# Plain units of the two branch products put singly between the retention's work, and all merge gates kept in DRAM

## The chip, the core and the metric

The kernel runs on one core of one Trainium2 chip. Five engines work side by side, each in the order of its own instruction stream: TensorE (PE in the profile: matmuls into PSUM; PEld is its weight load), VectorE (DVE), ScalarE (ACT), GpSimd (POOL) and SyncE (SP, used for DMA issues only). DMAs are issued by SP, ACT and POOL and carried out by 16 DMA engines. The metric is the device time of one execution in microseconds, as the median of several.

## The reference

Two layers (`DEPTH = 2`) over one sequence of 512 frames of width 1024, all in float32. What matters here is the part of a layer with two branches and their merge:

```python
y_m = sigmoid(mo) * head_layernorm(mlstm(mq, mk, mv, mi, mf))         # branch A, 4 heads
rq4 = rope(rq); rk4 = rope(rk) * R_DK ** -0.5                          # branch B, 4 heads
hr  = retention_chunkwise(rq4, rk4, rv, log_gamma)
y_r = silu(rg) * head_layernorm(hr)
merged = sigmoid(gm) * (y_m @ w_bm) + sigmoid(gr) * (y_r @ w_br)
x = x + merged @ w_out
```

`mq` to `gr` are columns of one projection of the normalised input. A feed-forward block and an embedding block follow in each layer, and a last normalisation.

## The kernel before

All activations are kept transposed: 128 features by 512 frames to a tile, eight tiles to the model's width. Every float32 operand is split into a high and a low part (`fp32r`), and a product is three matmuls: high by high, high by low, low by high (`mm3`, L450). The weights pass once, in the order of `unit_list` (L152), and each step of the computation takes the next unit from it:

- A plain unit (`T8`, function `t8`, L455) makes one output tile from one block of 1024 x 128 weights: 8 x 3 matmuls of 512 columns into one PSUM bank.
- A `PAIR` unit (`run_pair`, L482) makes two output tiles by a scheme of seven products P1, P5, P6, P2, P3, P7, P4 over half-size blocks, each of 12 matmuls of 256 columns, in three PSUM banks a, b and c (P1, P6, P7 and P4 share bank a; P5 and P3 share c). ScalarE evicts P1, P5, P6 and P4 to the two scratch tiles `y`, VectorE adds P2, P3 and P7 to them (`pair_tiles`, L556). P4 is not run at once: it is put on the list `later`, and `flush` (L477) runs it after P5 of the next pair, in the middle of the next plain unit (`k == 3`), or at the first row of an attention. Only then is the pair's result consumed.
- A `WIDE` unit (`run_wide`, L519) makes the retention's values of two heads.

Preparation of the weights: SP loads raw blocks into four buffers (`fill_raws`, L370); ScalarE rounds a block to its high part and VectorE subtracts it for the low part (`split`, L286), two pieces ahead of their use (`ready`, L440; `LOOK = 2`). A plain unit has one such piece of 1024 columns, a pair has pieces A, C and B of 1024 and D of 512 and some sums on VectorE. GpSimd forms further sums of weights from DRAM to DRAM, one step at a time as `pace` (L341) allows, from a credit that each unit adds to (`tick`, L345).

Scratch: `tmp` (L283) gives out tiles of 128 x 512 from one group of `NTMP = 6` slots. The pairs' `y`, the rotary work's `u` and `w` (L1082), the scores' `p`, the gates and the buffers of DRAM transfers all come from it.

A planner orders each engine's instructions ahead of time: it takes them by their place in the program, lets an engine take a later one when an earlier one isn't ready by its own estimates, and gives evictions of pairs a higher rank (`ahead`, L552). On the chip each engine then runs that fixed order and waits by semaphores.

The order around the change, in each layer (L1279 to L1332): the values of heads 0 and 1 (`rv_vals(0)`); four plain units of `y_m @ w_bm`; queries and keys of head 0 (`r_qk(0)`, two pairs, each followed by the rotary work); gate pair 2, `bm` units 4 and 5, gate pair 3, `bm` units 6 and 7; scores of head 0; `r_qk(1)`; attention of head 0 (`r_attend`, L1100); the fetch of head 1's values from DRAM (`rv_fetch`, L1212, issued by GpSimd into the buffers that the attention has just read); the first gate pair of head 0; the scores of head 1; and so on. `rv_split` splits the fetched values. `r_out` (L1120) makes a head's gate pairs, transposes the attention's result back and multiplies. After the attention of head 2 and the fetch for head 3 comes `r_qk(3)`, then eight plain units of the first half of `y_r @ w_br` (`br0`), the scores of head 3, and `r_out(2)`.

A merge gate of tiles 0 to 3 is made early by plain units (`gm_tile`, L1141) and stored to DRAM (`gm_spill`); `bm_tile` (L1286) loads it into scratch, multiplies the product's tile by it and stores the result (`bm_spill`). The gates of tiles 4 to 7 come from gate pairs 2 and 3 (`gm_gates`, L1133) and stay in their scratch tiles until `bm_tile` multiplies them in place.

Of the kernel before, what the change touches and what calls it, by code (L numbers as in the profile page):

```python
# [151 lines left out]
def unit_list(i):  # L152

    u = [("IF",)]

    def t8(w, col, row=0):
        u.append(("T8", w, row, col))

    def v(col):
        for k in range(4):  # L160
            u.append(("V", k, col))

    def pair(g, p):
        u.append(("PAIR", (i, g), p))

    def mqk(h):
        for d in range(2):
            t8("w_in", CQ + h * 256 + d * P)
        for d in range(2):
            t8("w_in", CK + h * 256 + d * P)  # L170

    def mo(h):
        for d in range(2):
            t8("w_in", CO + h * 256 + d * P)

    def rqk(h):
        for a in range(2):
            pair(f"rqk{h // 2 * 2}", h % 2 * 2 + a)

    def rg(h):  # L180
        for a in range(2):
            pair(f"rg{h // 2 * 2}", h % 2 * 2 + a)

    def full(w, col=0, row=0, lo=0, hi=8):
        for c in range(lo, hi):
            t8(w, col + c * P, row)

    mqk(0)
    v(CV)
    full("w_in", CGM, 0, 0, 2)  # L190
    mqk(1)
    mo(0)
    full("w_in", CGM, 0, 2, 3)
    mqk(2)
    mo(1)
    v(CV + 512)
    mqk(3)
    mo(2)
    full("w_in", CGM, 0, 3, 4)
    mo(3)  # L200
    u.append(("WIDE", (i, "rv0"), 0))
    full("w_bm", 0, 0, 0, 4)
    rqk(0)
    for p in (2, 3):
        pair("gm", p - 2)
        full("w_bm", 0, 0, 2 * p, 2 * p + 2)
    rqk(1)
    rg(0)
    u.append(("WIDE", (i, "rv2"), 0))
    rqk(2)  # L210
    rg(1)
    rqk(3)
    full("w_br")
    rg(2)
    rg(3)
    for p in range(4):
        pair("gr", p)
        full("w_br", 0, 1024, 2 * p, 2 * p + 2)
    full("w_out")

    def pairs(seq):
        for kind, b, p in seq:
            if kind == "f":
                t8("w_ff1", b * 1024 + 256 * p)
                t8("w_ff1", b * 1024 + 256 * p + P)
            else:
                pair(f"ff{b}", p)

    pairs(ff_order()[0])
    u.append(("PE", 0))  # L230
    pairs(ff_order()[1])
    u.append(("PE", 1))
    full("w_pe_gate")
    return u


def build(ctx, tc, ins, out):
# [25 lines left out]

    xs_dram = tc.dram_tile([KT, P, T], F32, name="x_spill")
    br_dram = tc.dram_tile([L, KT, P, T], F32, name="br_spill")
    gm_dram = tc.dram_tile([L, 4, P, T], F32, name="gm_spill")
    bm_dram = tc.dram_tile([L, KT, P, T], F32, name="bm_spill")
    rv_dram = tc.dram_tile([L, 2, NT, P, T], F32, name="rv_spill")

# [13 lines left out]
    def tmp(name, dt=F32):  # L283
        return cur["tmp"].tile([P, T], dt, name=name, tag="t", bufs=cur["ntmp"])
# [654 lines left out]
    for i in range(L):  # L939
# [129 lines left out]
        def m_back(h, gs, num):  # L1069
            gate_out(f"l{i}m{h}o", gs, num, [bcol(i, "gmn", 2 * h + v) for v in range(2)], ym, 2 * h)  # L1070

        def r_qk(h):
            nm = f"l{i}r{h}"
            qk = qk_tiles(nm)

# [14 lines left out]

            for a, bn in ((0, "brq"), (1, "brk")):
                pair_tiles(f"{nm}{bn}", xs, rope(a, bn))
            return qk

        def r_scores(h, qk):
# [15 lines left out]
        def r_gates(h, w, gs):  # L1111

            def consume(g):
                for d in range(2):
                    ac.activation(g[d], g[d], AF.Silu, bias=bcol(i, "brg", 4 * h + 2 * w + d), scale=SIGN[d])
                    gs[2 * w + d] = g[d]

            pair_tiles(f"l{i}r{h}o{w}", xs, consume)
# [14 lines left out]
        def gm_gates(p):  # L1133
            def consume(g):
                for d in range(2):
                    ac.activation(g[d], g[d], AF.Sigmoid, bias=bcol(i, "bgm", 2 * p + d), scale=SIGN[d])
                    gm[2 * p + d] = g[d]

            pair_tiles(f"l{i}bgm{p}", xs, consume)

# [98 lines left out]
                conv_evac(o, *a)  # L1239
        vv = mv_vals(0, xa, n1.c)  # L1240
        gct, gem = gate_cols(i, grow_c, grow_m)
        gm = {}
        for c in range(2):
            gm_tile(c, xa, n1)
        pt = m_scores(0, qk)
# [38 lines left out]
            nc.scalar.dma_start(t, ins[n])  # L1284

        def bm_tile(c):  # L1286
            if c < 4:
                gm[c] = tmp(f"l{i}gml{c}")
                nc.scalar.dma_start(gm[c], gm_dram[i, c])
            o = t8(ym, f"l{i}bm{c}")  # L1290
            g = gm.pop(c)
            ve.tensor_tensor(g, o, g, OP.mult)
            nc.scalar.dma_start(bm_dram[i, c], g)

        for c in range(4):
            bm_tile(c)
        qk = r_qk(0)
        for p in (2, 3):
            gm_gates(p)
            bm_tile(2 * p)  # L1300
            bm_tile(2 * p + 1)
        pt = r_scores(0, qk)
        qk = r_qk(1)
        num = r_attend(0, pt, vv)
        vv = rv_fetch(1)
        gs = {}
        r_gates(0, 0, gs)
        pt = r_scores(1, qk)
        rv_split(vv)
        yr = acts(cur["br"], f"l{i}yr0")  # L1310
# [7 lines left out]
        r_out(1, num, yr, gs)  # L1318
        num = r_attend(2, pt, vv)
        vv = rv_fetch(3)  # L1320
        qk = r_qk(3)
        for c in range(KT):
            o = t8(yr, f"l{i}br0{c}")
            t = tmp(f"l{i}brs{c}")
            ac.activation(t[:, :T], o, AF.Copy)
            nc.scalar.dma_start(br_dram[i, c], t[:, :T])
        pt = r_scores(3, qk)
        rv_split(vv)
        yr = acts(cur["br"], f"l{i}yr1")
        r_out(2, num, yr)  # L1330
        num = r_attend(3, pt, vv)
        r_out(3, num, yr)  # L1332
        mh, ml = [], []
# [365 lines left out]
```

## Time and profile before

| what | before |
|---|---|
| median of 3 runs | 2337.66 us (2335.55 to 2340.91) |
| profiled execution | 2338.24 us, its span 2336.5 us |
| TensorE busy | 2317.7 us (99%), 13664 matmuls |
| VectorE busy | 1722.3 us (74%) |
| ScalarE busy | 1224.1 us (52%) |
| GpSimd busy | 401.4 us (17%) |
| granted TensorE clock | 0.998 |
| DMA | 394.95 MB, mean 169 GB/s |

The span runs from the first to the last instruction of the profiled execution; a few microseconds of the time lie around it. A busy share is an average over the whole span. Matmuls are pipelined and their ends are modelled, so that each is drawn longer than the distance to the next one's start. A row of the waits names the waiting engine, its tile and line, who released it, and then the sum, the count and the longest. A row of a timeline gives start, duration, engine, line, operation, output and inputs, and in brackets the idle time before it and who ended it. Tile names begin with the layer (`l0`, `l1`) and the head (`r1` is head 1 of the retention, `m3` head 3 of the other branch); `o0` and `o1` are a head's two gate pairs, `brq` and `brk` its query and key pairs, `s` its scores, `a` its attention, `ot` the transposes back.

### The profile page before, as it was taken

How to read it: one execution, taken by the hardware profiler on the slowest of the kernel's cores; microseconds unless marked ns; L12 is line 12 of the kernel's file. 1: busy time of each engine (PE TensorE's matmuls, PEld its weight loads, DVE VectorE, ACT ScalarE, POOL GpSimd, SP SyncE). 2: the span in 40 equal slices, each digit the busy share in tenths (PEclk: the TensorE clock that was granted, in tenths of full speed). 3: DMA queues.
4: the chain of work that ended last, by engine and by line, in shares of the span. 5: the costliest groups of instructions: out<-in, count | busy, mean ns of one | idle time of the engine just before them, and what ended most of it. 6: DMA issues, size and time to landing. Idle time of an engine off the chain costs nothing.

```text
span 2336.5 us, 35728 instructions
## 1 busy us (share of the span) xinstructions
PE 2317.7 (99%) x13664; PEld 2055.3 (88%) x13664; DVE 1722.3 (74%) x2658; ACT 1224.1 (52%) x1771; POOL 401.4 (17%) x618
## 2 busy tenths in 40 slices
PE   9999999999999999999999999999999999999998
PEld 8888898898998898899888888998989988998997
DVE  7878767896665577678778777778957656776785
ACT  6756544554554445445557564454636445445464
POOL 3122212112114212112422221000000020000012
PEclk9999999999999999999999999999999999999999
DMA  6665886668688777777766666434443442333431
GB/s 214 166 172 155 249 230 183 195 176 224 176 239 253 197 205 191 206 203 189 212 177 172 154 178 196 145 121 151 129 138 114 157 154 99 127 109 94 136 122 55
DMA packets 150540, 394.95 MB, mean 169 GB/s; under 512 B 19344, under 2 KB 22800, under 8 KB 150368
## 3 DMA queue, kind: packets, MB, share of 16 engines
q1 hardware_dynamic: 99808, 247.50, 32.6%
q0 software_dynamic: 35152, 117.73, 22.9%
q10 hardware_dynamic: 15408, 27.43, 3.5%
q8 instruction: 107, 1.75, 0.3%
q14 instruction: 65, 0.53, 0.1%
HBM read 373.71 MB, written 123.73 MB: 213 GB/s over the span
## 4 chain that ended last, share of the span: by engine, by line
PE 84%; issue 6%; DVE 5%; DMA 2%; ACT 2%; POOL 1%; SPq 0%; ACTq 0%; DVEq 0%; POOLq 0%
PE l1f L451 2%; PE l0f L451 2%; PE l0f L452 2%; PE l1f L452 2%; PE l1f L453 2%; PE l0f L453 2%; PE l1br L451 1%; PE l0br L451 1%; PE l0br L453 1%; PE l1br L452 1%; PE l0br L452 1%; PE l1br L453 1%; PE l0pg L451 1%; PE l0pg L453 1%; PE l1bm L451 1%
## 5 line engine op out<-in xcount | busy, mean ns | idle before, releaser
L287 ACT ACTIVATE wh<-wr 128x1024 fp32r<-128x1024 f32 (+1 forms) x223 | 231.2, 1044 | 286.4 <-issue 62.9
L288 DVE TENSOR_TENSOR wl<-wr,wh 128x1024 fp32r<-128x1024 f32 (+1 forms) x221 | 272.4, 1234 | 73.7 <-ACT wh L287 73.5
L287 ACT ACTIVATE wh_B<-wr 128x1024 fp32r<-128x1024 f32 x100 | 105.9, 1059 | 149.8 <-PE l1bm L452 13.1
L288 DVE TENSOR_TENSOR wl_B<-wr,wh_B 128x1024 fp32r<-128x1024 f32 x100 | 122.0, 1220 | 20.8 <-ACT wh_B L287 20.8
L287 ACT ACTIVATE wh_C<-wr 128x1024 fp32r<-128x1024 f32 x76 | 80.3, 1057 | 64.4 <-issue 9.6
L287 ACT ACTIVATE wh_D<-wr 128x512 fp32r<-128x512 f32 x76 | 48.0, 631 | 124.8 <-DVE wr L433 57.2
L288 DVE TENSOR_TENSOR wl_A<-wr,wh_A 128x1024 fp32r<-128x1024 f32 x76 | 92.8, 1221 | 20.2 <-ACT wh_A L287 20.2
L288 DVE TENSOR_TENSOR wl_C<-wr,wh_C 128x1024 fp32r<-128x1024 f32 x76 | 94.3, 1241 | 16.1 <-ACT wh_C L287 15.7
L287 ACT ACTIVATE wh_A<-wr 128x1024 fp32r<-128x1024 f32 x76 | 80.0, 1052 | 47.2 <-PE l0f L452 6.7
L451 PE MATMUL l1f<-l1n2h,wh 128*128 128x512 f32 x256 | 99.9, 390 | 0.0
L451 PE MATMUL l0f<-l0n2h,wh 128*128 128x512 f32 x256 | 99.8, 390 | 0.0
L453 PE MATMUL l0f<-l0n2h,wl 128*128 128x512 f32 x256 | 99.7, 389 | 0.0
L453 PE MATMUL l1f<-l1n2h,wl 128*128 128x512 f32 x256 | 99.7, 389 | 0.0
L452 PE MATMUL l0f<-l0n2l,wh 128*128 128x512 f32 x256 | 99.6, 389 | 0.0
L452 PE MATMUL l1f<-l1n2l,wh 128*128 128x512 f32 x256 | 99.6, 389 | 0.0
L288 DVE TENSOR_TENSOR wl_D<-wr,wh_D 128x512 fp32r<-128x512 f32 x76 | 52.5, 690 | 36.9 <-ACT wh_D L287 35.8
L662 POOL TENSOR_TENSOR l1n3sum<-l1n3sum,l1n3sq 128x512 f32<-128x512 f32 x6 | 9.2, 1539 | 330.8 <-ACT l1n3sum L654 309.8
L430 DVE TENSOR_TENSOR wr<-wr,wr 128x512 f32<-128x512 f32 x76 | 52.2, 687 | 16.2 <-DMA wr<-wpairs 15.3
L453 PEld LDWEIGHTS l1f<-l1n2h,wl 128*128 128x128 f32 x256 | 48.0, 188 | 10.1
L453 PEld LDWEIGHTS l0f<-l0n2h,wl 128*128 128x128 f32 x256 | 48.0, 188 | 10.0
L452 PEld LDWEIGHTS l0f<-l0n2l,wh 128*128 128x128 f32 x256 | 48.1, 188 | 9.9
L452 PEld LDWEIGHTS l1f<-l1n2l,wh 128*128 128x128 f32 x256 | 48.1, 188 | 9.8
(5626 smaller groups left out, 8558.3 us busy)
## 6 DMA issues: line engine op xcount, KB each, us to landing
wr<-wstream SPq DMA_DIRECT2D x219, 512.0 KB, 4.5
wr<-wpairs SPq DMA_DIRECT2D x228, 256.0 KB, 3.0
wr<-wwide SPq DMA_DIRECT2D x24, 512.0 KB, 3.7
s0t<-wwide POOLq DMA_DIRECT2D x10, 512.0 KB, 5.6
s4t<-wwide POOLq DMA_DIRECT2D x10, 512.0 KB, 6.4
s12t<-wwide POOLq DMA_DIRECT2D x10, 512.0 KB, 5.4
s16t<-wwide POOLq DMA_DIRECT2D x10, 512.0 KB, 5.5
s1t<-wpairs POOLq DMA_DIRECT2D x16, 256.0 KB, 4.1
```

The lines of the kernel that those rows point to most:

```text
L287: a = ac.activation(hi_ap, src, AF.Copy)
L288: return a, ve.tensor_sub(lo_ap, src, hi_ap.bitcast(F32))
L430: ve.tensor_tensor(raws[n, "B"][:, Q:], kept.pop((n, "A"))[:, Q:], r[:, :Q], OP.add)
L451: te.matmul(o, sh, mh, start=first, stop=False)
L452: te.matmul(o, sh, ml, start=False, stop=False)
L453: cur["mm"] = te.matmul(o, sl, mh, start=False, stop=last)
L662: (add or gp).tensor_tensor(self.sum, self.sum, sq, OP.add)
```

## The change

The plain units of `y_m @ w_bm` and of the first half of `y_r @ w_br` are no longer run in blocks. The new order of a layer is: `bm` 0 and 1, `r_qk(0)`, gate pair 2, `bm` 2, gate pair 3, `bm` 3, scores 0, `bm` 4, first pair of `r_qk(1)`, `bm` 5, second pair, `bm` 6, attention 0 and fetch, first gate pair of head 0, `bm` 7, scores 1. Later: attention 2 and fetch, `br0` 0, first pair of `r_qk(3)`, `br0` 1 and 2, second pair, `br0` 3 and 4, scores 3, `br0` 5, `rv_split`, first gate pair of head 2, `br0` 6 and 7, `r_out(2)` with its other gate pair. `unit_list` gives the weights in the same order, and `r_qk` takes a function that it calls between its two pairs.

All eight merge gates now pass through DRAM: `gm_gates` stores its two tiles to `gm_spill`, which grows from 4 to 8 tiles per layer, and `bm_tile` loads every gate. Both DMAs are issued by ScalarE. The number of matmuls and of operations on VectorE and ScalarE is the same; each layer has four stores and four loads of 256 KB more.

```diff
@@ unit_list
-    full("w_bm", 0, 0, 0, 4)
+    def bm(c, n=1):
+        full("w_bm", 0, 0, c, c + n)
+
+    def br(c, n=1):
+        full("w_br", 0, 0, c, c + n)
+
+    bm(0, 2)
     rqk(0)
-    for p in (2, 3):
-        pair("gm", p - 2)
-        full("w_bm", 0, 0, 2 * p, 2 * p + 2)
-    rqk(1)
-    rg(0)
+    pair("gm", 0)
+    bm(2)
+    pair("gm", 1)
+    bm(3, 2)
+    pair("rqk0", 2)
+    bm(5)
+    pair("rqk0", 3)
+    bm(6)
+    pair("rg0", 0)
+    bm(7)
+    pair("rg0", 1)
     u.append(("WIDE", (i, "rv2"), 0))
     rqk(2)
     rg(1)
-    rqk(3)
-    full("w_br")
-    rg(2)
+    br(0)
+    pair("rqk2", 2)
+    br(1, 2)
+    pair("rqk2", 3)
+    br(3, 3)
+    pair("rg2", 0)
+    br(6, 2)
+    pair("rg2", 1)
     rg(3)
@@ build
-    gm_dram = tc.dram_tile([L, 4, P, T], F32, name="gm_spill")
+    gm_dram = tc.dram_tile([L, KT, P, T], F32, name="gm_spill")
@@ r_qk
-        def r_qk(h):
+        def r_qk(h, mid=None):
...
             for a, bn in ((0, "brq"), (1, "brk")):
                 pair_tiles(f"{nm}{bn}", xs, rope(a, bn))
+                if mid and not a:
+                    mid()
@@ gm_gates
                     ac.activation(g[d], g[d], AF.Sigmoid, bias=bcol(i, "bgm", 2 * p + d), scale=SIGN[d])
-                    gm[2 * p + d] = g[d]
+                    nc.scalar.dma_start(gm_dram[i, 2 * p + d], g[d])
@@ the layer
         def bm_tile(c):
-            if c < 4:
-                gm[c] = tmp(f"l{i}gml{c}")
-                nc.scalar.dma_start(gm[c], gm_dram[i, c])
+            g = tmp(f"l{i}gml{c}")
+            nc.scalar.dma_start(g, gm_dram[i, c])
             o = t8(ym, f"l{i}bm{c}")
-            g = gm.pop(c)
             ve.tensor_tensor(g, o, g, OP.mult)
             nc.scalar.dma_start(bm_dram[i, c], g)
-        for c in range(4):
-            bm_tile(c)
+        bm_tile(0)
+        bm_tile(1)
         qk = r_qk(0)
-        for p in (2, 3):
-            gm_gates(p)
-            bm_tile(2 * p)
-            bm_tile(2 * p + 1)
+        gm_gates(2)
+        bm_tile(2)
+        gm_gates(3)
+        bm_tile(3)
         pt = r_scores(0, qk)
-        qk = r_qk(1)
+        bm_tile(4)
+        qk = r_qk(1, lambda: bm_tile(5))
+        bm_tile(6)
         num = r_attend(0, pt, vv)
         vv = rv_fetch(1)
         gs = {}
         r_gates(0, 0, gs)
+        bm_tile(7)
         pt = r_scores(1, qk)
...
-        qk = r_qk(3)
-        for c in range(KT):
-            o = t8(yr, f"l{i}br0{c}")
-            t = tmp(f"l{i}brs{c}")
-            ac.activation(t[:, :T], o, AF.Copy)
-            nc.scalar.dma_start(br_dram[i, c], t[:, :T])
+        def br_tiles(*cs):
+            for c in cs:
+                o = t8(yr0, f"l{i}br0{c}")
+                t = tmp(f"l{i}brs{c}")
+                ac.activation(t[:, :T], o, AF.Copy)
+                nc.scalar.dma_start(br_dram[i, c], t[:, :T])
+
+        yr0 = yr
+        br_tiles(0)
+        qk = r_qk(3, lambda: br_tiles(1, 2))
+        br_tiles(3, 4)
         pt = r_scores(3, qk)
+        br_tiles(5)
         rv_split(vv)
+        gs = {}
+        r_gates(2, 0, gs)
+        br_tiles(6, 7)
         yr = acts(cur["br"], f"l{i}yr1")
-        r_out(2, num, yr)
+        r_out(2, num, yr, gs)
```

More of the change, by code (lines that the diff above doesn't have):

```diff
@@ L1241, in build @@
         gct, gem = gate_cols(i, grow_c, grow_m)
-        gm = {}
         for c in range(2):
```

## The prediction

> **What bounds the kernel now.** I read the page first (busy time by engine, then the span in 40 slices), then TensorE's waits, then the two stretches that the change rewrites, then the waits one by one on the timelines of TensorE, ScalarE and VectorE.
>
> ```profile
> span 2336.5 us, 35728 instructions
> PE 2317.7 (99%) x13664; PEld 2055.3 (88%) x13664; DVE 1722.3 (74%) x2658; ACT 1224.1 (52%) x1771; POOL 401.4 (17%) x618
> PE   9999999999999999999999999999999999999998
> PEclk9999999999999999999999999999999999999999
> ```
>
> TensorE is busy in every slice at the full granted clock, and the change removes and adds no matmul: the floor stays. What can move is only TensorE's idle time, and the list of its waits is short:
>
> ```profile
> PE l0r0o0c L501 <- ACT l0r0o0y L571: 2.0, 1, 2.0
> PE l1r0o0c L501 <- ACT l1r0o0y L571: 1.7, 1, 1.7
> ...
> PE l0r2o1a L501 <- DVE l0r2o1y L579: 0.7, 1, 0.7
> ...
> PE l1r3brqa L501 <- ACT l1r3brqy L569: 0.6, 1, 0.6
> PE l0r3brqa L501 <- ACT l0r3brqy L569: 0.6, 1, 0.6
> ...
> PE l1r2o1a L501 <- DVE l1r2o1y L579: 0.3, 1, 0.3
> ...
> 285.30:654.20 368.90, 365.63 (x2417) 335.88 (x2416) 277.31 (x416) 186.49 (x288) 69.23 (x103) 1.00 0.72 198
> 1442.60:1811.40 368.80, 366.18 (x2420) 336.35 (x2420) 278.19 (x417) 186.84 (x289) 12.03 (x20) 1.00 0.42 133
> ```
>
> The last two rows are the changed stretches, from the first `bm` unit to the first `br1` unit of each layer: length, then busy TensorE, weight loads, VectorE, ScalarE, GpSimd, then clock and DMA share. Six waits lie in them, 2.0 + 1.7 + 0.7 + 0.6 + 0.6 + 0.3 = 5.9 us, and the two rows' own idle agrees (3.27 + 2.62 = 5.9). Idle understates a stall, since a matmul's modelled end lies behind the start of the next:
>
> ```profile
> 402.62 0.28 PE L501 MATMUL l0r0o0a<-l0xsh,wh_B 128*128 128x256 f32 x1
> 402.74 0.28 PE L502 MATMUL l0r0o0a<-l0xsl,wh_B 128*128 128x256 f32 x1
> ...
> 403.33 0.40 PE L452 MATMUL l0r1s<-l0r1ql,l0r1kh 128*128 128x512 f32 x1
> 403.56 0.39 PE L453 MATMUL l0r1s<-l0r1qh,l0r1kl 128*128 128x512 f32 x1
> 405.90 0.38 PE L501 MATMUL l0r0o0c<-l0xsh,wh_C 128*128 128x256 f32 x1 [1.95 <-ACT l0r0o0y L571]
> ```
>
> Two matmuls of 512 columns start 0.23 us apart although each is drawn 0.39 us long (256 columns: 0.12 and 0.28), so each wait costs 0.16 us more than it shows: 5.9 + 6 x 0.16 = 6.9 us (0.3%). That is the most that the change can gain.
>
> **What each wait is made of.** In the first pair after `attend(0)` TensorE waits for ScalarE to evict product P5, and ScalarE was busy waiting for the four value tiles fetched from DRAM:
>
> ```profile
> 402.91 1.30 ACT L287 ACTIVATE l0r1vh<-l0r1vl 128x512 fp32r<-128x512 f32 x2 [0.84 <-DMA l0r1vl<-rv_spill]
> 404.95 0.63 ACT L287 ACTIVATE l0r1vh<-l0r1vl 128x512 fp32r<-128x512 f32 x1 [0.74 <-DMA l0r1vl<-rv_spill]
> 405.49 0.36 ACT L571 ACTIVATE l0r0o0y<-l0r0o0c 128x256 f32<-128x256 f32 x1
> ...
> 403.14 1.19 DVE L288 TENSOR_TENSOR wl_B<-wr,wh_B 128x1024 fp32r<-128x1024 f32 x1
> ...
> 391.40:406.00 14.60, 12.65 (x76) 10.76 (x74) 13.60 (x25) 8.36 (x15) 5.14 (x9) 1.00 0.52 174
> ```
>
> The fourth row shows a second cause: the pair's weights B got their low half only at 403.14 + 1.19 = 404.33, because VectorE was busy 13.60 of 14.60 us with the rotary work of head 1. With B late, TensorE's order leaves P6 (two matmuls done, the third, which needs the low half, due at 402.86) and P2, does three of the next scores and then goes to P3, which needs the late eviction. In `rqk3` it is ScalarE again, behind a fetched tile:
>
> ```profile
> 527.35 0.63 ACT L287 ACTIVATE l0r3vh<-l0r3vl 128x512 fp32r<-128x512 f32 x1 [0.69 <-DMA l0r3vl<-rv_spill]
> ```
>
> **The change, part by part.** A plain unit is 24 matmuls of 512 columns, 24 x 0.227 = 5.45 us (0.23 above, 45.0 us for eight units and a product below) of TensorE, and leaves VectorE and ScalarE nearly free: over the block of eight `br0` units VectorE is busy 45%, over the pairs behind it 72%:
>
> ```profile
> 545.20:590.20 45.00, 45.00 (x206) 37.49 (x205) 20.41 (x25) 14.04 (x19) 10.50 (x16) 1.00 0.85 216
> 594.10:616.80 22.70, 21.97 (x186) 21.70 (x185) 16.40 (x26) 13.47 (x24) 3.91 (x6) 1.00 0.72 187
> ```
>
> (1) `br0` unit 0 now stands between `attend(2)` with its fetch and the first `rqk3` pair. The splits of the fetched tiles wait behind 5.45 us of matmuls that need no eviction; the late landing was worth 0.6 us. Both waits go: 2 x (0.6 + 0.16) = -1.5 us.
>
> (2) `br0` units 6 and 7 stand between the two gate pairs of head 2: 10.9 us in which VectorE catches up before the product that waited for its add. -(0.7 + 0.16) - (0.3 + 0.16) = -1.3 us. What is late next there is nothing that the rows show.
>
> (3) `bm` unit 6 stands ahead of `attend(0)`, so head 1's rotary work starts 5.45 us sooner against the attention and the B weights (late by 404.33 - 402.86 = 1.5 us) are ready. P6 and P2 then run whole, 24 matmuls of 0.12 us = 2.9 us from 402.62, and P3 is due at 405.5 instead of 403.8. The eviction still ends at 405.49 + 0.36 = 405.85: 0.4 us stay of 2.0 + 0.16. The fetch itself is not moved, so I do not take the whole: -(2.1 - 0.4) - (1.9 - 0.4) = -3.2 us. From both sides: 0 if ScalarE's order moves with it, -4.0 if the landing comes 0.4 us sooner.
>
> (4) Four more gates per layer are stored and fetched by way of ScalarE's queue, 16 transfers in all. Issue costs 0.33 us each, 16 x 0.33 = 5.3 us of an engine that is idle 48% of the time: nothing on the path. The fetch and the two stores hold scratch slots, of which there are six:
>
> ```profile
> L1289 ACTq DMA_DIRECT2D l0gml<-gm_spill x4: 326/330/396, 245.8 to 271.3; - x4
> DMA to landing us min/median/max: 2.6/5.6/8.9
> ...
> L1293 ACTq DMA_DIRECT2D bm_spill<-l1gml x4: 326/326/327, 1449.0 to 1465.3; - x4
> DMA to landing us min/median/max: 2.0/2.1/4.0
> ...
> L1326 ACTq DMA_DIRECT2D br_spill<-l0brs x8: 326/326/333, 553.8 to 591.8; - x8
> DMA to landing us min/median/max: 4.7/5.0/5.3
> ```
>
> Before, the loads of gates 0 to 3 were issued 14 us or more ahead of their use. Unit `bm` 2 now follows gate pair 2 as unit 4 did before, and there the key's rotary scratch is given back late:
>
> ```profile
> 335.68 0.40 PE L451 MATMUL l0bm<-l0ymh,wh 128*128 128x512 f32 x1
> ...
> 339.08 0.69 DVE L1086 TENSOR_TENSOR l0r0brku<-l0r0brku,l0r0brkw 128x512 f32<-128x512 f32 x1
> ...
> L1289 ACTq DMA_DIRECT2D l1gml<-gm_spill x4: 326/329/402, 1403.1 to 1428.7; - x4
> DMA to landing us min/median/max: 2.0/2.7/2.7
> ```
>
> All six slots are taken until 339.08 + 0.69 = 339.8, 4.1 us into the unit; only then can its gate be asked for. It lands 2.6 to 8.9 us later in layer 0, and 2.0 to 2.7 in layer 1 (the last row). The multiply waits on VectorE, the store behind it on ScalarE, and the next evictions queue behind both. The unit with the product inside it has 2.8 us left, and the next pair runs 2.8 us before P6 wants its bank again, less 1.1 for multiply and eviction: 4.5 us of slack. That is 0 to 4.4 us in layer 0, 1.1 by the median, and nothing in layer 1. VectorE has room there, so I take 0.5.
>
> The Trainium skill, page DMA: Bandwidth & Descriptors, section Anatomy of one DMA (SWDGE path), fits one transfer as about 2.0 us and the bytes at 436 GB/s, an estimated 2.6 us for 256 KB. It matches layer 1's rows and is below layer 0's; by it this term would be zero and the sum 0.5 us lower.
>
> (5) `bm` unit 5 inside `rqk1` has a price that the blocks did not have. The first pair's P4 is flushed in the middle of the unit, so the rotary scratch u, w, u, w is asked for before the second pair's y. Scratch is given out in program order:
>
> ```profile
> 663.88 0.69 DVE L1354 TENSOR_TENSOR l0bml<-l0bml,l0brl 128x512 f32<-128x512 f32 x1
> ...
> 669.63 0.38 ACT L571 ACTIVATE l0gr1y<-l0gr1c 128x256 f32<-128x256 f32 x1 [0.97 <-PE l0gr1c L503]
> 669.69 0.33 ACTq L1348 DMA_DIRECT2D l0brl<-br_spill  x1
> ...
> 320.56 0.37 ACT L581 ACTIVATE l0r0brqy<-l0r0brqa 128x256 f32<-128x256 f32 x1
> 326.62 0.74 DVE L1085 SCALAR_TENSOR_TENSOR l0r0brqw<-l0r0brqy,bc,l0cos 128x512 f32<-128x512 f32 x1
> ```
>
> The scratch of `brl` was last read at 664.57, yet the next load into scratch comes at 669.69, right behind the pair's second y, which precedes it in the program. The last two rows give the rotary work's own time: its last scratch, the second w, is taken 326.62 - 320.56 = 6.1 us after the eviction of P4. In `rqk1` the second pair's P1 must be evicted 4.9 us after it: half a unit, 2.7, and two products of 1.4, less 0.4 for the eviction and 0.2 for P4's own tail. It costs 6.1 - 4.9 = 1.2 us if VectorE is as full as there, nothing if the unit frees it, and I allow twice that, 2.5, where the unit's own store still holds a slot. I take 1.2 per layer, the case that the rows show: +2.4 us. `rqk3` has two units between its pairs, so there it costs nothing.
>
> Sum: -1.5 - 1.3 - 3.2 + 0.5 + 2.4 = -3.1 us. The profiled execution took 2338.24 us (span 2336.5 and 1.7 around it), 0.6 above the median of the runs, 2337.66. From the median: 2334.6 us. A measurement of this kernel tells about 0.2%, 4.7 us, from no change; the sum is inside that.
>
> **Rivals.** First, all six waits go and none comes: 2337.66 - 6.9 = 2330.8 us. For it: every wait stands where a plain unit is put, and VectorE and ScalarE have room. Against it: the fetch of `attend(0)` is not moved. It is faster once 4.7 of the 6.9 us are kept.
>
> Second, slower: the scratch slots. If a y must take the slot of a store that has not landed, each such place costs the landing less the 1.4 us of slack, 5.0 - 1.4 = 3.6 us by the stores of `br0` in layer 0. The places are three per layer: gates 6 and 7, the second pair of `rqk1`, the second pair of `rqk3`. Three in layer 0 are +10.8; with the -6.0 of (1) to (3) that is 2342.5, and with layer 1's three at 4.0 - 1.4 = 2.6 it is 2350. I put it at 2344. It decides from 10.7 us of new waits on. For it: six slots, and a stage that now keeps one of them for a gate all the time. Against: before, gates 4 to 7 sat in their slots for a whole pair and two units, which is longer.
>
> Third, the change moves the waits and not their sum: ScalarE's splits come ahead of evictions elsewhere, and the time is 2337.7. For it: the order within each engine is planned ahead, from transfer times that the real landings exceed (the 0.84 and 0.74 us above).
>
> **How the numbers follow.** The forecast of 2334.6 (its own range 2333.0 to 2337.0) has 0.36, the third rival 0.07; both are no change: 0.43. The first has 0.27, faster. The second has 0.30, slower, since its price has the widest bounds. The range reaches from the first rival, 2330.8, less 0.8 for the spread between runs, to 2344.5 and leaves out the second's upper part, under 0.2.
>
> **What would show it.** Right: TensorE's waits no longer list `r3brq` and `r2o1`, `r0o0c` stays under 0.6, and a wait at `r1brk`'s first eviction appears. (3) is wrong if `r0o0c` is still 2.0; (5) if `r1brk` shows no gap. The prediction fails if waits of ScalarE on `gm_spill`, `bm_spill` or `br_spill` end gaps of TensorE of several us.

## The result and the profile after

The changed kernel takes 2343.55 us in the median of 20 runs (2337.38 to 2347.3), the kernel before 2339.3 us beside it, also of 20: a ratio of 1.002, with an interval of 1.0013 to 1.0026. It is slower by 0.2%, 4.3 us by the medians, where 3.1 us less was forecast. The profiled execution took 2343.51 us, its span 2341.8: 5.3 us more than the span before. TensorE is as busy as it was; these are the page's first lines and TensorE's waits in the changed stretches:

```profile
span 2341.8 us, 35732 instructions
PE 2321.0 (99%) x13664; PEld 2056.8 (88%) x13664; DVE 1725.2 (74%) x2658; ACT 1225.4 (52%) x1771; POOL 402.2 (17%) x618
...
PE l0bgm3a L518 <- ACT l0bgm3y L586: 2.4, 1, 2.4
PE l0r0o0a L518 <- ACT l0r0o0y L586: 2.3, 1, 2.3
PE l1r3brqa L520 <- DVE wl_B L305: 1.3, 1, 1.3
PE l0r3brqa L520 <- DVE wl_B L305: 1.1, 1, 1.1
...
PE l0r1brkc L518 <- ACT l0r1brky L588: 0.5, 1, 0.5
PE l1r1brkc L518 <- ACT l1r1brky L588: 0.5, 1, 0.5
```

The six waits of before are gone in their old form; six others have come. With 0.16 us added to each, as in the prediction, layer 1 gains: 0.66 + 1.46 new against 1.86 + 0.76 + 0.46 old is -0.96 us. Layer 0 loses: 2.56 + 2.46 + 1.26 + 0.66 against 2.16 + 0.86 + 0.76 is +3.2, and each of its two long stalls has a second price. The next rows are the same view as the stretches of the prediction (length, busy time of TensorE, weight loads, VectorE, ScalarE, GpSimd, then granted clock, DMA share, GB/s), for two times two neighbouring pieces of 3.4 us:

```profile
333.66:337.07 3.41, 1.30 (x12) 1.09 (x10) 1.27 (x2) 0.17 (x1) 0.00 (x0) 1.00 1.00 371
337.08:340.48 3.40, 3.15 (x14) 3.15 (x15) 2.63 (x5) 2.23 (x5) 0.00 (x0) 0.50 0.61 234
...
401.93:405.34 3.41, 1.09 (x10) 0.89 (x9) 3.32 (x8) 2.18 (x5) 0.57 (x1) 1.00 0.82 218
405.35:408.75 3.40, 3.40 (x19) 3.40 (x18) 2.46 (x6) 2.40 (x5) 2.07 (x2) 0.50 0.76 271
```

Behind either stall the clock is granted at 0.50 for 3.4 us, so up to half of that, 1.7 us, is lost again: at most 3.2 + 2 x 1.7 = +6.6 in layer 0, and 5.6 with layer 1, against 5.3 by the spans. Before, no piece inside the kernel ran at half clock.

**The stall in gate pair 3 of layer 0.** VectorE and ScalarE, from their timelines:

```profile
335.80 0.69 DVE L1308 TENSOR_TENSOR l0gml<-l0bm,l0gml 128x512 f32<-128x512 f32 x1 [4.37 <-DMA l0gml<-gm_spill]
...
326.73 0.33 ACTq L1306 DMA_DIRECT2D l0gml<-gm_spill  x1
...
336.53 0.33 ACTq L1309 DMA_DIRECT2D bm_spill<-l0gml  x1
336.90 0.38 ACT L586 ACTIVATE l0bgm3y<-l0bgm3a 128x256 f32<-128x256 f32 x1 [3.92 <-DVE l0gml L1308]
...
DMA to landing us min/median/max: 2.6/2.8/9.0
```

Gate 2 is asked for at 326.73, when the slots come free, and lands 9.0 us later (the last row: issue to landing of those of the 16 gate loads whose landing the trace tells; this is the longest). VectorE waits 4.37 us for it, the store of the product behind it on ScalarE, and the pair's first eviction behind that store.

**The stall in the first gate pair of head 0, layer 0,** begins ten microseconds earlier, at another late transfer:

```profile
386.09 0.79 POOL L353 DMA_DIRECT2D s5t<-wpairs  x1 [5.67 <-PE l0r1brka L520]
...
386.34 0.33 SPq L404 DMA_DIRECT2D wr<-wpairs  x1
...
393.00 0.69 DVE L447 TENSOR_TENSOR wr<-wr,wr 128x512 f32<-128x512 f32 x1 [5.04 <-DMA wr<-wpairs]
393.62 0.74 DVE L1101 SCALAR_TENSOR_TENSOR l0r1brku<-l0r1brky,bc,l0cos 128x512 f32<-128x512 f32 x1
...
402.44 0.69 DVE L450 TENSOR_TENSOR wr<-wr 128x512 f32<-128x512 f32 x1
...
403.16 0.63 ACT L304 ACTIVATE wh_D<-wr 128x512 fp32r<-128x512 f32 x1 [2.77 <-DVE wr L450]
...
404.22 0.36 ACT L586 ACTIVATE l0r0o0y<-l0r0o0a 128x256 f32<-128x256 f32 x1
```

VectorE's order has the sum of a freshly loaded weight ahead of head 1's key rotation. The load was issued at 386.34, 0.25 us behind one of GpSimd's weight sums (the first row), and VectorE waits 5 us for it. All that is queued behind it moves: the rotation, then the sum for piece D at 402.44, ScalarE's rounding of D, and the eviction that TensorE waits for.

### The profile page after: what moved, and what is told of

Its sections match the earlier page's. It is cut to its first block, busy times and chain, and to the rows that moved or that the text cites. A ratio compares the mean times of both kernels' runs of the same rounds, so it can differ in the third digit from the quotient of the medians.

```text
span 2341.8 us, 35732 instructions
## 1 busy us (share of the span) xinstructions
PE 2321.0 (99%) x13664; PEld 2056.8 (88%) x13664; DVE 1725.2 (74%) x2658; ACT 1225.4 (52%) x1771; POOL 402.2 (17%) x618
## 4 chain that ended last, share of the span: by engine, by line
PE 87%; DVE 6%; issue 3%; DMA 2%; ACT 1%; POOL 0%; ACTq 0%; DVEq 0%; SPq 0%; POOLq 0%
PE l1f L468 2%; PE l0f L468 2%; PE l0f L469 2%; PE l1f L469 2%; PE l1f L470 2%; PE l0f L470 2%; PE l0br L468 1%; PE l0br L470 1%; PE l0br L469 1%; PE l1br L468 1%; PE l1br L470 1%; PE l1br L469 1%; PE l0pg L468 1%; PE l0pg L470 1%; PE l1wo L469 1%
## 5 line engine op out<-in xcount | busy, mean ns | idle before, releaser
L468 PEld LDWEIGHTS l0f<-l0n2h,wh 128*128 128x128 f32 x256 | 48.1, 188 | 9.8
```

The lines of the kernel that those rows point to most:

```text
L468: te.matmul(o, sh, mh, start=first, stop=False)
```

## The experiments

Each run was timed in five rounds (two_sums in one) against the kernel before on the same chip, most with 11 executions, gate_early with 5, dummy_after with 6 and two_sums with 7; "us" is the difference of the medians, in brackets the interval of the ratio. The table has TensorE's waits in us, layer 0 / layer 1, with "-" where none is listed, and the stretches of half clock inside the kernel. The columns are the pairs at which TensorE waits: `bgm3` is gate pair 3, `r1brk` head 1's key pair, `r0o0` the first gate pair of head 0, `r3brq` head 3's query pair, `r2o1` the second gate pair of head 2.

| run | us | bgm3 | r1brk | r0o0 | r3brq | r2o1 | half clock |
|---|---|---|---|---|---|---|---|
| before | 0 | - / - | - / - | 2.0 / 1.7 | 0.6 / 0.6 | 0.7 / 0.3 | 0 |
| changed | +4.3 [1.0013, 1.0026] | 2.4 / - | 0.5 / 0.5 | 2.3 / - | 1.1 / 1.3 | - / - | 2 |
| bm_only | +2.3 [0.9996, 1.0014] | 0.7 / - | 0.5 / 0.5 | 3.5 / - | 0.3 / - | 1.2 / 0.3 | 1 |
| br_only | +1.9 [1.0002, 1.002] | - / - | - / - | 2.1 / 2.7 | 1.1 / 1.3 | - / - | 1 |
| nosum_before | -3.9 [0.9975, 0.9992] | - / - | - / - | 1.8 / 1.4 | - / - | 0.3 / 0.4 | 0 |
| nosum_after | -4.1 [0.9975, 0.9992] | - / - | 0.5 / 0.5 | - / 0.2 | 0.8 / 1.1 | - / - | 0 |
| gate_early | +13.0 [1.0037, 1.0062] | 5.5 / 2.1 | 0.5 / 0.5 | 3.3 / - | 1.3 / 1.1 | 0.2 / - | 3 |
| br0_later | +4.6 [1.0009, 1.0027] | 0.5 / - | 0.6 / 0.5 | 2.3 / - | 0.2 / - | 1.9 / 0.3 | 1 |
| bm5_out | +1.5 [0.9994, 1.0013] | 2.3 / - | - / - | 1.4 / 1.4 | 1.1 / 1.0 | - / - | 1 |
| sums_paused | +5.4 [1.0014, 1.0031] | - / - | 4.2 / 0.5 | - / - | 1.2 / 1.2 | 0.3 / - | 2 |
| dummy_before | +4.5 [1.0007, 1.0025] | - / - | - / - | 1.5 / 2.0 | 0.5 / - | 0.9 / 0.3 | 1 |
| dummy_after | +10.6 [1.003, 1.006] | 2.3 / - | 0.7 / 1.6 | 3.1 / - | 1.5 / 1.0 | 0.3 / - | 3 |
| one_copy | +4.5 [1.001, 1.0027] | 2.3 / - | 1.0 / 0.5 | 0.7 / - | 1.1 / 1.3 | - / - | 1 |
| two_sums | +8.1 [1.0026, 1.0051] | 1.7 / 1.6 | 0.5 / 0.5 | 2.7 / - | 1.4 / 0.9 | - / - | 2 |
| mix | -1.6 [0.9983, 1.0] | - / - | - / - | 0.9 / 0.8 | 0.7 / - | 1.3 / 0.3 | 0 |
| mix_paused | -1.1 [0.9987, 1.0004] | - / - | - / - | 0.9 / 0.9 | - / - | 0.3 / 0.3 | 1 |
| mix_bm | -3.5 [0.9977, 0.9995] | - / - | - / - | 0.3 / 0.8 | 0.6 / 0.8 | 0.9 / 0.3 | 0 |
| mix_br | +3.3 [1.0005, 1.0023] | - / - | - / - | 1.6 / 2.2 | 0.7 / - | 1.8 / 0.4 | 1 |

The waits are those of one execution, and the landings differ from one to the next: layer 1's `r0o0` is 2.7 us in br_only and 1.7 before, although layer 1 has the same order up to there. The time is the safer column.

### The two halves

```diff
 # bm_only: the br0 units as before
+    rqk(3); full("w_br"); rg(2); rg(3)
-    br(0); pair("rqk2", 2); br(1, 2); pair("rqk2", 3); br(3, 3); pair("rg2", 0); br(6, 2); ...
 # br_only: the bm units as before, gates 4 to 7 kept in scratch
+    bm(0, 4); rqk(0)
+    for p in (2, 3):
+        pair("gm", p - 2); bm(2 * p, 2)
+    rqk(1); rg(0)
```

> The bm half alone: the order of the eight bm units and the gates by way of DRAM as in the changed kernel, the eight br0 units in one block behind rqk3 as before. Theory A (the loss is made by late DMA landings in layer 0, at gate 2 of the merge and at the weights ahead of r0o0, each stall with a few us of half clock behind it): the whole loss stays, +4 to +7 us against the kernel before, with TensorE's waits at l0bgm3 and l0r0o0a over 2 us each and a half clock behind them, none in layer 1. Rival B (the loss comes from br0 unit 0 ahead of rqk3 and the other places of br0): within 2 us of the kernel before. Under both, the waits at r3brq stay as they were before (0.6 us each, on ScalarE).

> The br0 half alone: the order of the eight br0 units and of head 2's gates as in the changed kernel, the bm units in blocks and gates 4 to 7 kept in scratch as before. Theory A: r3brq gets worse by 0.6 to 0.8 us per layer, r2o1 better by 0.9 and 0.5, so -0.5 to +0.8 us, no difference to be measured. Rival B: +4 to +6 us. The step of the prediction that put -1.5 us on r3brq would give -2.8 with r2o1.

Theory A is met in neither run: the bm half should have kept +4 us or more and the br half should have cost nothing to be measured. By the medians each costs about half of the loss, +2.3 and +1.9 us, but bm_only's interval holds no change, so rival B is not ruled out by its time. In the bm half it is layer 0's `r0o0`, 3.5 us with a half clock behind; `bgm3` waits 0.7 us here, since gate 2 landed sooner. In the br half `r3brq` is worse as expected and `r2o1` is gone; its one half clock stands behind layer 0's `r0o0`, a place that this run does not change and where the kernel before waits about as long without one, so part of its +1.9 us may be chance.

### Without the weight sums

Of the two changed stretches, GpSimd's sums of weights from DRAM to DRAM run in that of layer 0 (GpSimd is busy 69 us of it and 12 of layer 1's, by the prediction's rows); in layer 1 they end ahead of it. In these two runs none is made, and another given block is loaded where a sum was.

```diff
-        return given[g, x] if x in GIVEN else sums[g, x]
+        return given[g, x] if x in GIVEN else given[g, "B12"]
...
-        dma = gp.dma_start(flat(block(g, x)[p:p + 1]), flat(block(g, MADE[x][a])[p:p + 1]), ...)
```

> The kernel before without the DRAM-to-DRAM weight sums on GpSimd's queue; another given block is loaded where a sum was, so the loads are the same and the output is not the reference's. This is the base for the next run. Both theories: -1 to -6 us against the kernel before (it is idle 18.8 us in all, and no matmul goes), with the r0o0c wait of layer 0 still there, since layer 1, which has few sums, has it as well (1.7 against 2.0 us).

> The changed kernel without the weight sums, in the same way (output not the reference's). Compare with the run without sums of the order before. Theory A: the waits of over 2 us at l0bgm3 and l0r0o0a are gone, no half clock in that stretch, layer 0 gains about what layer 1 gained (0.9 us), so -1 to -2 us against the order before. Rival C (the loss is the planned order on the engines and the scratch slots, whatever the DMA traffic): +4 to +6 us stay, and both waits stay over 2 us.

The loss is gone: 2334.86 us against 2335.13. So are both long stalls and the half clock, and layer 0 now looks as layer 1 does. The changed kernel's two stretches, and the same without sums:

```profile
285.00:660.00 375.00, 368.67 (x2410) 338.20 (x2410) 278.12 (x414) 186.94 (x288) 69.70 (x103) 0.99 0.72 202
1440.00:1815.00 375.00, 373.14 (x2442) 341.32 (x2441) 283.33 (x420) 190.09 (x291) 13.43 (x22) 1.00 0.43 141
```

```profile
285.00:660.00 375.00, 373.58 (x2455) 342.14 (x2454) 281.38 (x418) 191.11 (x294) 12.30 (x20) 1.00 0.45 142
1440.00:1815.00 375.00, 373.22 (x2454) 341.90 (x2453) 281.44 (x418) 191.03 (x293) 12.35 (x20) 1.00 0.44 142
```

That the loss needs the sums is shown. It is not a wait for a sum to be finished: the two late loads, of `gm_spill` and `wpairs`, carry none. Theory A's gain of 1 to 2 us is not shown: without late landings the change is worth 0.3 us, less than can be told. The waits moved and their sum stayed, which is the prediction's third rival.

### What makes gate 2 late, and whether asking earlier helps

```diff
 # gate_early
+        g2 = gate_load(2)
         gm_gates(2)
-        bm_tile(2)
+        bm_tile(2, g2)
```

> The changed kernel with the load of merge gate 2 issued ahead of gate pair 2 instead of behind it, one pair (about 8 us) earlier in the program. Theory A1 (the 2.5 us gap at l0bgm3 is the late landing of that gate): the gap there goes, with the half clock behind it, -2.5 to -4.0 us in layer 0 against the changed kernel, 2339.5 to 2341 us. Rival A2 (the gap is a scratch slot: the load holds one and the pair's y must wait for it, wherever the load stands): a gap of over 1 us stays in gate pair 2 or 3, and the time is within 1.5 us of the changed kernel.

A1 falls, and A2 with it: it is far worse than either. The load now takes the slot that the key's rotation needs, and the rotation waits for the store of the gate:

```profile
335.73 0.75 DVE L1102 SCALAR_TENSOR_TENSOR l0r0brkw<-l0r0brky,bc,l0sin 128x512 f32<-128x512 f32 x1 [8.22 <-DMA gm_spill<-l0bgm2y]
```

The store was issued at 326.89 and lands at the same time as the load did in the changed kernel, 335.7. In both orders one transfer must land within about a unit, the load or the store; with six slots the order chooses which. Layer 1 now stalls too (1.7 and 0.4 us), where no sums run: that is the price of the slots alone.

Can the sums step aside?

```diff
 # sums_paused
-        if at["step"] < len(steps) and at["credit"] >= 0:
+        if at["step"] < len(steps) and at["credit"] >= 0 and not cur.get("hold"):
...
+        cur["hold"] = i == 0
         gm_gates(2); bm_tile(2); gm_gates(3)
+        cur["hold"] = False
         bm_tile(3); ...; qk = r_qk(1, lambda: bm_tile(5))
+        cur["hold"] = i == 0
         bm_tile(6); ...; r_gates(0, 0, gs)
+        cur["hold"] = False
```

> The changed kernel, all sums made, but in layer 0 none is started from gate pair 2 to gate pair 3 and from the middle of rqk1 to the first gate pair of head 0; the credit that is saved up starts them behind. The theory as it stands after the earlier runs (a transfer of 256 KB that is due within one unit lands 5 to 9 us late while sums run, whether it is the gate's load, its store or a weight): both stalls of over 2 us (l0bgm3a, l0r0o0a) and their half clocks go, -5 to -8 us against the changed kernel, 2335.5 to 2338.5. Rival (a total of traffic in the layer is what counts, the pauses move the late landings to other places): within 2 us of the changed kernel.

Both stalls go, as the theory says, and the time stays, as the rival says. The sums that were saved up come between the pauses, and the same chain forms there, one pair earlier:

```profile
374.41 0.69 DVE L447 TENSOR_TENSOR wr<-wr,wr 128x512 f32<-128x512 f32 x1 [6.26 <-DMA wr<-wpairs]
...
377.72 0.63 ACT L304 ACTIVATE l0r1qh<-l0r1brqu 128x512 fp32r<-128x512 f32 x1 [4.00 <-DVE l0r1brqu L1103]
378.26 0.36 ACT L586 ACTIVATE l0r1brky<-l0r1brka 128x256 f32<-128x256 f32 x1
```

The opposite test puts the traffic into layer 1:

```diff
 # dummy_before, dummy_after: in layer 1, at the pace of the sums
+        dma = gp.dma_start(flat(spare[k // 2 % 8]), flat(given[g, "B12"][k % 2:k % 2 + 1]), **kw)  # 256 KB, every other one accumulating
 # one_copy: two plain copies of 512 KB at gate pair 2 of layer 1
+        cur["copies"] = [(0, wide, "B12", 0)] + [None] * 6 + [(1, wide, "B12", 1)] if i else []
 # two_sums: the same with accumulations into them, the last at the end of gate pair 2
+        cur["copies"] = [(1, wide, "B12", 1), (0, wide, "B22", 0, add)] + [None] * 5 + [(1, wide, "B22", 1, add)] if i else []
```

> The same 88 copies in layer 1 of the kernel before. Theory A: the old order has its loads and stores far enough ahead, so layer 1 becomes what layer 0 is there: +0 to +1.5 us (l1r0o0c, r3brq and r2o1 up by 0.1 to 0.4 us each), and the gap between the two orders grows from 4.3 to 8 us or more. Rival: the copies cost both orders alike.

> The changed kernel with the traffic of layer 0 put into layer 1 too: 88 more DRAM-to-DRAM copies and accumulations of 256 KB on GpSimd's queue, at the pace of the sums, from the first bm unit to the last gates of head 3; nothing reads them. Theory A: layer 1 now shows layer 0's stalls (at l1bgm3a and l1r0o0a, over 2 us, some with a half clock): +4 to +9 us against the changed kernel, and +8 to +13 against the kernel before; the run with the same copies in the order before is the base. Rival (layer 0's losses come from something else of that layer): +0 to +2 us, layer 1's waits as they were.

> The changed kernel with just two more copies of 512 KB from DRAM to DRAM on GpSimd's queue, in layer 1, where layer 0 has two such sums: one at the start of gate pair 2 and one at its end, right ahead of the load of gate 2 for unit bm 2. The 88 copies of 256 KB spread over layer 1 left l1bgm3a without a wait. Theory W (a wide copy that starts just ahead of a load that is due within one unit is what makes the stall, not the amount of traffic in the layer): layer 1's gate 2 lands 5 us or later after its issue (2 to 4.4 us in the changed kernel) and l1bgm3a waits 1 us or more. Rival (it takes the whole traffic of layer 0, weights, sums and spills together): it lands under 4.5 us and l1bgm3a has no wait over 0.3 us. The time tells little: +0 to +4 us against the changed kernel.

> The changed kernel with two whole wide sums on GpSimd's queue in layer 1, at the places of layer 0's: two copies of 512 KB from DRAM to DRAM and, behind them, two accumulations of 512 KB into them, the last right ahead of the load of gate 2; nothing reads the result. The plain copy of the last run left that load on time. Theory W2 (an accumulation, which reads its target and writes it again, is what holds the transfers up): layer 1's gate 2 lands 5 us or later and l1bgm3a waits 1 us or more. Rival (it takes the rest of layer 0's traffic as well): under 4.5 us and no wait over 0.3 us.

The 88 transfers of 256 KB miss what theory A expected: they cost the order before 4.5 us, not 0 to 1.5, and the gap between the two orders is 6.1 us, not 8 (dummy_after's six executions spread over 12 us, so the two are not told apart). Layer 1's `bgm3` and `r0o0a` stay without a wait; only its `r1brk` goes from 0.5 to 1.6 us. The profiled execution, the slowest of the six, also has a wait of 3.7 us at `l1bgm` with a half clock. It lies at 1280 us, ahead of the first added transfer at 1458, so the traffic does not make it. In one_copy the plain copies leave gate 2 on time. In two_sums, with the accumulations, the stall comes to layer 1, here on ScalarE:

```profile
1489.06 0.33 ACTq L1315 DMA_DIRECT2D l1gml<-gm_spill  x1
...
1498.15 0.33 ACTq L1318 DMA_DIRECT2D bm_spill<-l1gml  x1
1498.53 0.38 ACT L595 ACTIVATE l1bgm3y<-l1bgm3a 128x256 f32<-128x256 f32 x1 [3.16 <-DVE l1gml L1317]
```

So two wide sums, the last accumulation issued at 1488.00, about a microsecond ahead of a transfer due within one unit, are enough, and the amount of traffic in a layer is not. This rests on one execution of each. A narrow accumulation ahead of that load was not tried; in dummy_after one is issued 0.4 us behind it, and the load is on time. That a narrow one can do it too is suggested by the late weight ahead of layer 0's `r0o0`: the sum issued 0.25 us before it is one of 256 KB, and its issue takes 0.79 us, like the accumulations of two_sums (0.84) and unlike plain copies (0.53). The multiply began 8.4 us after the load's issue; the profile puts its wait down to a product that it does not read, so that landing is inferred.

### Steps 1, 2 and 5

```diff
 # br0_later
-    br(0)
     pair("rqk2", 2)
-    br(1, 2)
+    br(0, 3)
 # bm5_out
-    bm(5)
     pair("rqk0", 3)
-    bm(6)
+    bm(5, 2)
```

> The changed kernel with br0 unit 0 put behind the first pair of rqk3 instead of ahead of it (pair, br0 0 to 2, pair). Theory S (the unit ahead of the pair keeps the weight buffers, so that the pair's B weights get their low half too late): the waits for wl_B at r3brq (1.1 and 1.3 us) go, and at most the 0.6 us on ScalarE of the kernel before comes back: -0.6 to -1.4 us per layer, -1.2 to -2.8 us against the changed kernel. Rival (VectorE has too much to do after attend(2), whatever stands ahead of the pair): the waits for wl_B stay within 0.3 us.

> The changed kernel with bm unit 5 behind the second pair of rqk1 instead of between its two pairs. Step 5 of the prediction (scratch in program order makes the second pair's y wait): the gaps of 0.68 us at r1brk go in both layers, -1.4 us. The second reading (the gap at l0r0o0a comes from a late weight load that VectorE's order waits for, and that is late by the traffic): that gap can go either way in layer 0, 1.5 to 4 us, since the loads are not moved; if two units ahead of attend(0) instead of one make it vanish, VectorE's backlog was the cause and not the load.

Theory S holds for the wait and not for the time. In the changed kernel the unit ahead of the pair keeps a weight buffer until its last matmul, so ScalarE rounds B only then, and by then VectorE's order has the head's scaling and two splits ahead of B's low part:

```profile
538.46 1.06 ACT L304 ACTIVATE wh_B<-wr 128x1024 fp32r<-128x1024 f32 x1 [0.25 <-PE l0br L469]
...
538.54 1.92 DVE L834 TENSOR_SCALAR l0r2num<-l0r2num,l0r2mv,l0r2hv 128x512 f32<-128x512 f32 x4 [0.94 <-POOL l0r2hv L1126]
540.37 1.28 DVE L305 TENSOR_TENSOR l0r3vl<-l0r3vl,l0r3vh 128x512 fp32r<-128x512 f32 x2
541.58 1.22 DVE L305 TENSOR_TENSOR wl_B<-wr,wh_B 128x1024 fp32r<-128x1024 f32 x1
```

With the unit behind the pair, both waits for `wl_B` are gone, but `r2o1`'s are back (1.9 and 0.3), with the units 6 and 7 still between the gate pairs. VectorE of layer 1, in br0_later and then in the changed kernel:

```profile
1773.68 0.69 DVE L446 TENSOR_TENSOR wr<-wr,wr 128x512 f32<-128x512 f32 x1 [0.62 <-DMA wr<-wpairs]
1774.29 0.42 DVE L593 TENSOR_TENSOR l1r2o1y<-l1r2o1c,l1r2o1y 128x256 f32<-128x256 f32 x1
1774.62 1.22 DVE L304 TENSOR_TENSOR wl_C<-wr,wh_C 128x1024 fp32r<-128x1024 f32 x1
1775.75 0.42 DVE L595 TENSOR_TENSOR l1r2o1y<-l1r2o1a,l1r2o1y 128x256 f32<-128x256 f32 x1
```

```profile
1773.96 1.23 DVE L305 TENSOR_TENSOR wl_C<-wr,wh_C 128x1024 fp32r<-128x1024 f32 x1 [0.38 <-ACT wh_C L304]
1775.10 0.42 DVE L594 TENSOR_TENSOR l1r2o1y<-l1r2o1c,l1r2o1y 128x256 f32<-128x256 f32 x1
1775.43 0.68 DVE L447 TENSOR_TENSOR wr<-wr,wr 128x512 f32<-128x512 f32 x1
1776.03 0.42 DVE L596 TENSOR_TENSOR l1r2o1y<-l1r2o1a,l1r2o1y 128x256 f32<-128x256 f32 x1
```

In the first the sum of a weight, whose load has just not landed, stands ahead of both adds; in the second it stands between them, where it no longer waits. In layer 0 the same instruction waits 2.21 us in br0_later. So the wait goes with the place of that sum in VectorE's order.

Unit 5 behind the second pair takes `r1brk`'s gap away in both layers, as step 5 has it. The gap is not a wait for scratch, though. ScalarE in the changed kernel:

```profile
379.29 0.63 ACT L304 ACTIVATE l0r1qh<-l0r1brqu 128x512 fp32r<-128x512 f32 x1 [1.03 <-DVE l0r1brqu L1103]
...
379.83 0.36 ACT L588 ACTIVATE l0r1brky<-l0r1brkc 128x256 f32<-128x256 f32 x1
```

The second pair's P1 is evicted at 377.88, right behind its last matmul. What TensorE waits for is P5's eviction, which stands in ScalarE's order behind the rounding of head 1's query; ScalarE waits 1.03 us for VectorE's rotation there. Layer 1 shows the same. With unit 5 behind the pair, layer 0's `r0o0` shrinks to 1.4 us and layer 1's comes back with 1.4, though another unit now stands ahead of the attention: there ScalarE waits 1.94 us for a fetched value tile, and the eviction is behind its rounding.

### A version that beats both

```diff
 # mix_bm: the kernel before, except
-    for p in (2, 3): pair("gm", p - 2); full("w_bm", 0, 0, 2 * p, 2 * p + 2)
-    rqk(1)
+    pair("gm", 0); bm(4, 2); pair("gm", 1); bm(6)
+    rqk(1)
+    bm(7)                   # its gate alone by way of DRAM
 # mix_br: the kernel before, except
+    pair("rqk2", 2); br(0, 3); pair("rqk2", 3); br(3, 3); pair("rg2", 0); br(6, 2); pair("rg2", 1)
 # mix: both; mix_paused: mix with pauses of the sums at attend(0) to r0o0 and at head 2's gates
```

> Made of the parts that looked right: the bm units in the blocks of before, except that unit 7 stands behind rqk1, ahead of attend(0), with its gate by way of DRAM (the other gates as before); the br0 units 0 to 2 between the pairs of rqk3, 6 and 7 between the gate pairs of head 2. Theory A: r2o1's waits go (-0.9 and -0.5), layer 1's r0o0c goes (-1.9), r3brq -0.3 to +0.3 each, r1brk has no gap, l0bgm3 has none; layer 0's r0o0 between -2.1 and +2 us by the landing of the weights. In sum -5.4 to -1.3 us against the kernel before, 2333.5 to 2337.6. Rival (whatever stands ahead of attend(0) costs layer 0 as much as it gains layer 1, with a half clock): 0 to +2 us.

> The mixed order with pauses of the sums in layer 0 ahead of and at attend(0) to the first gate pair of head 0, and at head 2's gate pairs. Theory: the waits at l0r0o0a (0.9) and l0r2o1a (1.3) shrink by half or more, -1 to -2 us against the mixed order, 2334.5 to 2336.5. Rival (the pauses only move late landings): within 0.7 us of the mixed order.

> The bm half of the mixed order alone: bm 7 ahead of attend(0) with its gate by way of DRAM, everything else as in the kernel before. If the mixed order's gain is from this half: -1 to -2.5 us against the kernel before (r0o0's stalls of 2.1 and 1.9 become about 1.0 each). If it is from the br0 half: within 0.7 us.

> The br0 half of the mixed order alone: units 0 to 2 between the pairs of rqk3, 3 and 4 ahead of the scores, 5 behind them, 6 and 7 between the gate pairs of head 2; bm as before. The third rival of the prediction (waits move and their sum stays): r3brq's 0.75 go, r2o1's 0.5 to 2 stay, within 1 us of the kernel before. By the prediction's steps 1 and 2 it would be -2.8 us.

The bm half of the mix is the gain: 2335.54 us against 2339.03, a ratio of 0.9986 with 0.9977 to 0.9995, more than the 1 to 2.5 us expected. Its waits:

```profile
PE l0r2o1a L509 <- DVE l0r2o1y L587: 0.9, 1, 0.9
PE l1r3brqa L509 <- ACT l1r3brqy L577: 0.8, 1, 0.8
...
PE l0r3brqa L509 <- ACT l0r3brqy L577: 0.6, 1, 0.6
PE l1r0o0a L509 <- DVE l1r0o0y L587: 0.4, 1, 0.4
...
PE l1r0o0a L509 <- ACT l1r0o0y L577: 0.4, 1, 0.4
PE l0r0o0a L509 <- ACT l0r0o0y L577: 0.3, 1, 0.3
...
PE l1r2o1a L509 <- DVE l1r2o1y L587: 0.3, 1, 0.3
```

One unit ahead of `attend(0)` takes `r0o0` from 2.0 and 1.7 to 0.3 and 0.8, and one gate through DRAM, stored two pairs ahead of its use, makes no new wait. The br0 units between pairs lose by themselves even with unit 0 put right, 3.3 us where the rival had less than 1 and steps 1 and 2 a gain of 2.8: layer 1's `r3brq` gains, and layer 0's `r2o1` goes to 1.8 us with a half clock behind it. The pauses are worth nothing that can be told (-1.1 against -1.6 us for the mix without them), though `r2o1` in layer 0 falls from 1.3 to 0.3 us; mix_paused's half clock stands behind a wait of 3.5 us at `l1bgm`, far from the pauses.

## Why the prediction was wrong, step by step

By the waits of the two profiled executions the steps come to +1.2 for (1), -1.3 for (2), +0.3 and -1.9 for (3) in layers 0 and 1, +2.6 for (4) and +1.3 for (5), in sum +2.2 us where -3.1 was forecast; up to 3.4 of half clock, which the prediction put at nothing, come on top. The steps that failed most are (1), (3) in layer 0, (4) and the clock; all but (1) go away without the sums.

(1) Wrong. It looked at ScalarE, which the unit does relieve, and not at the weight buffers that the unit itself holds: instead of -1.5 the waits went to `wl_B`, 1.1 and 1.3 us, about +1.2 in all.

(2) Right in size (-1.3; both waits left the list), by luck, since its reason is wrong. VectorE had room before as well; what stood ahead of the add was a weight sum waiting for its load. br0_later has the same two units there and the wait.

(3) Right in layer 1, where the whole 1.7 + 0.16 went (1.5 was forecast). In layer 0 the wait became another of the same size, from a weight that landed 5 us late. The prediction named late landings for the gates and put none on the weights.

(4) The place, the chain and the mechanism are as it said; the term of 0.5 us was mis-sized. The landing was 9.0 us, at the upper end that it had noted (8.9), and the stall 2.4 + 0.16. With up to 1.7 of half clock that makes 4.3 us, and that this meets its bound of 4.4 is luck: the bound has no half clock in it, and it took the load to be asked for 4.1 us into the unit, where it was asked for at 1.7 (326.73; the unit's first matmul is at 325.01). Taking the median landing of a layer was the error: what counts is the landing at that moment, and two_sums points to an accumulating sum just ahead. By the estimate of the Trainium skill (page DMA: Bandwidth & Descriptors, section Anatomy of one DMA (SWDGE path)), 2.6 us, the gate would have been on time; layer 1's loads are near that, this one is 3.5 times as long. That section is about transfers issued by GpSimd, and these are issued by ScalarE.

(5) Right in place, in both layers, and gone in bm5_out; 0.66 us per layer instead of 1.2. The cause was not the scratch: the second w was taken 3.0 us after the eviction of P4 (376.71 against 373.70), not 6.1, and P1's eviction came on time. It was the first pair's rotary work on VectorE, which ScalarE's order waits for ahead of P5's eviction. The rows that it read as scratch in program order, the load at 669.69, show a load that stands behind an eviction in ScalarE's order, which is enough to explain it.

The rivals: the third holds once the sums are left out (-0.3 us). The second is what the scratch slots do in gate_early; that its 2344 lies beside the 2343.55 measured is luck, for none of the changed kernel's six waits is for the slot of a store. None counted the half clock, since before none of the stalls had one.

What stays open: why an accumulating sum holds a transfer up where a plain copy does not, and whether a narrow one is enough; why the added traffic costs the order before 4.5 us although its listed waits hardly grow; and the 0.1% that the br0 half costs, of which the waits of the profiled executions explain only a part.

## What to carry to other kernels

When the bound engine is 99% busy, moving filler work moves waits; before counting a wait as gone, look at what stands next in the fixed order of the engine that releases it, and whether that is an instruction that depends on a DMA. Price a transfer by the slowest landing in its neighbourhood and not by the median of its kind, and give it more lead than that or leave its tile where it is. Move one unit at a time: of all that were moved, the one ahead of `attend(0)` carries the gain.

## What the runs showed that was not expected

The clock. After some stalls TensorE ran for one stretch of 3413 ns (in the trace's record of the granted clock; in sums_paused for two such stretches on end, in gate_early for three) at half clock, which costs up to 1.7 us, nearly as much as the stall. All these stretches begin on one grid of 3413 ns that runs through the whole execution, and whether a stall has one depends on how it lies on the grid. Pieces of the kernel before, then of gate_early:

```profile
401.99:405.39 3.40, 1.96 (x14) 1.49 (x12) 3.01 (x6) 1.78 (x4) 1.56 (x4) 1.00 0.87 290
405.41:408.80 3.39, 2.90 (x24) 2.90 (x25) 2.52 (x5) 0.83 (x3) 0.81 (x1) 1.00 0.12 47
```

```profile
407.48:410.88 3.40, 0.09 (x2) 0.02 (x1) 3.31 (x8) 1.49 (x4) 0.00 (x0) 1.00 0.98 263
410.90:414.29 3.39, 3.39 (x28) 3.39 (x29) 2.45 (x5) 3.35 (x7) 2.64 (x3) 1.00 0.73 235
```

I take as idle what lies between the start of a matmul, plus its usual 0.12 or 0.23 us, and the start of the next. Before, the stall in the first row lies across the grid and leaves one piece of it idle for 47%: full clock. In the changed kernel the two pieces with the stalls (quoted with the result) are idle for 67 and 76%: half clock in the next. In gate_early a stretch of 3.4 us with hardly a matmul in it, the first of its two rows, is split by the grid into 54 and 50%: full clock behind it, in the second row. Over all 18 profiles, each of the 20 pieces that were idle for 58% or more has a half clock behind it, and none of those with 56% or less. Where the line lies between the two depends on this way of counting idle. The Trainium skill (page TensorE: Matmul & The Clock Gate, section What's actually happening) has a free-running window of 3413 ns, and the traces agree. The same page of the Trainium skill, section HAM oscillation, warns of gaps above about 3.4 us; here 2.0 us within one window (58%) were enough, and 3.4 us across two were not.
